# A two-layer diffusion step on one core: the engines' instruction order planned with the framework's other simulator

## The chip, the cores and the metric

One core of a Trainium2 chip runs the whole program. The metric is the device time of one execution in microseconds, the median over several runs; lower is better.

## The reference

One inference step of a hybrid diffusion backbone in float32 with two layers, the first with differential attention, the second with multi-head latent attention. 1024 latent tokens (`x_sample`) attend to themselves and to 256 cached tokens; 256 context tokens (`x_prompt`) attend to themselves alone. Both layers have 8 heads, a model width of 1024, RMS norms around them and an adaptive shift, scale and gate.

```python
for i in range(DEPTH):                       # DEPTH = 2
    hc = rmsnorm(x_ctx, g_pre[i]) * (1 + sc_c) + sh_c
    hl = rmsnorm(x_lat, g_pre[i]) * (1 + sc_l) + sh_l
    if kind == 0:                            # differential attention
        q, k, v, gate = split(h @ da_w_in)   # rope on q, k of the latents; cached k, v appended
        p = softmax(q k^T * scale)           # two score maps per head
        w = p[:, :, 0] - lam * p[:, :, 1]
        o = rmsnorm(w @ v, g_sub) * (1 - lam_init) * silu(gate)
    else:                                    # multi-head latent attention
        q_a, kv_a, k_pe, gate = split(h @ mla_w_in)
        q = rmsnorm(q_a, g_qa) @ w_qb ;  k, v = rmsnorm(kv_a, g_kva) @ w_kvb
        o = softmax([q_nope, q_pe] [k_nope, k_pe]^T * scale) @ v * silu(gate)
    x = x + gate_i * rmsnorm(o @ w_out[i], g_post[i])
```

It returns both streams and the new keys, values and latents of the context tokens.

## The kernel before

Each float32 operand of a large product is split into a high part and a remainder, and `mm3` (L320 on) issues three TensorE products for one: high by high (L323), and the two mixed ones (L324, L325). Weights come in through SyncE's queue (L313), ScalarE makes the high part (L315), and GpSimd or VectorE the remainder (L316; L355 and L356 for the query and key weights of the first layer). The 1280 rows are five pairs of 128-row tiles, four of latents and one of context tokens.

The time falls into five stages, which the text below calls A to E:

- A: norms and transposes of the inputs (`norm_pair_to_hT`, L286 to L295), the adaptive parameters, and the query, key and first value projections of layer 1 (`l0_qk_item`, `l0_tok_item`).
- B: the heads of layer 1 (`l0_heads`). A unit of work is one 128-row tile of one head, nine of them per head, 72 in all. `l0_scores` computes two score maps in PSUM tiles `S` (L594) and `pj` (L602), takes their maximum (L596) and the exponentials (L608, L610); `l0_weigh` mixes the two maps (L639); `p_transpose` transposes them (L662) and splits them into `pth` and `ptl` (L664, L665); `l0_values` multiplies with the values (by `mm3`) and stores through L699. The scores are recorded two units ahead of the weights. Between them a `Feeder` records further projections (values, gates, adaptive parameters, the first chunks of the gated output).
- C: the output projection of layer 1 (`out_items`, `residual`), the norms and transposes of layer 2 (L286 to L295 again) and its input projections (`l1_items`).
- D: the heads of layer 2 (`l1_heads`), 80 units: scores (`l1_scores`, L1255 to L1259), maximum and exponential (L1270 to L1274), transposes and splits as before, values (`l1_values`, L1297, L1298), with the projections of the next head between them.
- E: the output projection of layer 2 and the final sums (L980, L986).

The kernel is recorded, not issued: leaving the tile context hands the whole list to the framework's planner. The planner runs the list through a simulator of the core. Whenever that simulator can take another instruction on an engine, the planner gives it the earliest recorded one whose inputs and buffers are free at that simulated moment; later recorded work passes work that is not ready. What comes out is one fixed order for every engine and for every queue that issues transfers, with semaphores between them. On the chip each engine keeps to its order.

So the order in which the program is recorded sets priorities, and the planner's simulated clock sets who overtakes whom. How finely two recorded streams can mix is visible in one loop of `l0_heads`:

```python
for w in f[:2]:
    next(turns)          # transposes and splits of this unit
    feed(w)              # projection work, as much as the weight w allows
    next(sc, None)       # scores two units ahead
```

No line of the kernel fixes the order by hand beyond this: there are no explicit semaphores and no manual dependencies.

## Time and profile before

| | |
|---|---|
| median of 3 runs | 2020.48 us (2020.45 to 2022.48) |
| the profiled execution, own time | 2026.26 us |
| its span, first to last instruction | 2024.3 us |
| mean granted TensorE clock | 0.985 |
| TensorE busy, weight loads busy | 1925.5 us, 1729.8 us |
| VectorE, ScalarE, GpSimd busy | 1255.1, 965.1, 520.4 us |
| bytes moved by DMA | 225.05 MB, mean 111 GB/s |

The profiled execution is 5.8 us longer than the median. The profile counts an instruction as busy from its start to its end; matmuls are pipelined, so consecutive ones overlap and the busy time of TensorE is the union of them. Idle time of an engine is put down to what released the instruction that ended it.

### The profile page before, as it was taken

How to read it: one execution, taken by the hardware profiler on the slowest of the kernel's cores; microseconds unless marked ns; L12 is line 12 of the kernel's file. 1: busy time of each engine (PE TensorE's matmuls, PEld its weight loads, DVE VectorE, ACT ScalarE, POOL GpSimd, SP SyncE). 2: the span in 40 equal slices, each digit the busy share in tenths (PEclk: the TensorE clock that was granted, in tenths of full speed). 3: DMA queues.
4: the chain of work that ended last, by engine and by line, in shares of the span. 5: the costliest groups of instructions: out<-in, count | busy, mean ns of one | idle time of the engine just before them, and what ended most of it. 6: DMA issues, size and time to landing. Idle time of an engine off the chain costs nothing. (4 is left out here: it accounts for less than half of the span.)

```text
span 2024.3 us, 36143 instructions
## 1 busy us (share of the span) xinstructions
PE 1925.5 (95%) x13472; PEld 1729.8 (85%) x13472; DVE 1255.1 (62%) x2511; ACT 965.1 (48%) x2421; POOL 520.4 (26%) x741
## 2 busy tenths in 40 slices
PE   6899999999999999999988899999999999999998
PEld 4788888798989787888888898888999889998998
DVE  4544456788878787898337533247766876777413
ACT  4421223567666666667345523234554444545421
POOL 3354443213122212223334431011000110003214
PEclk8999999999999999999999999999999999999999
DMA  8455643544455454456434312210100001013412
GB/s 307 143 164 184 189 158 131 159 132 139 125 148 170 127 160 130 132 161 192 152 110 129 97 35 74 81 42 26 31 28 28 22 26 39 27 38 94 150 62 104
DMA packets 211440, 225.05 MB, mean 111 GB/s; under 512 B 24033, under 2 KB 175937, under 8 KB 211137
## 3 DMA queue, kind: packets, MB, share of 16 engines
q1 hardware_dynamic: 210960, 222.70, 35.6%
q8 instruction: 106, 1.74, 0.4%
q14 instruction: 70, 0.57, 0.1%
q10 hardware_dynamic: 304, 0.05, 0.0%
HBM read 153.14 MB, written 69.53 MB: 110 GB/s over the span
## 5 line engine op out<-in xcount | busy, mean ns | idle before, releaser
L323 PE MATMUL pj<-wh,hh 128*128 128x256 f32 (+1 forms) x1264 | 370.4, 293 | 8.9 <-DVE ptl L665 3.5
L324 PE MATMUL pj<-wl,hh 128*128 128x256 f32 (+1 forms) x1264 | 360.8, 285 | 6.1 <-DVE wl L316 3.7
L325 PE MATMUL pj<-wh,hl 128*128 128x256 f32 (+1 forms) x1264 | 360.3, 285 | 1.7 <-POOL hl L295 1.6
L316 POOL TENSOR_TENSOR wl<-wst,wh 128x512 fp32r<-128x512 f32 (+3 forms) x98 | 113.0, 1161 | 582.2 <-ACT wh L315 485.8
L323 PEld LDWEIGHTS pj<-wh,hh 128*128 128x128 f32 x1264 | 243.6, 193 | 14.4 <-DVE ptl L665 4.1
L324 PEld LDWEIGHTS pj<-wl,hh 128*128 128x128 f32 x1264 | 243.9, 193 | 8.2 <-DVE wl L316 4.1
L325 PEld LDWEIGHTS pj<-wh,hl 128*128 128x128 f32 x1264 | 243.3, 193 | 4.3 <-POOL hl L295 3.0
L325 PE MATMUL pj<-hh,wl 128*128 128x512 f32 (+1 forms) x512 | 188.5, 368 | 0.6 <-POOL wl L356 0.5
L323 PE MATMUL pj<-hh,wh 128*128 128x512 f32 (+1 forms) x512 | 188.3, 368 | 0.0
L324 PE MATMUL pj<-hl,wh 128*128 128x512 f32 (+1 forms) x512 | 187.8, 367 | 0.0
L596 DVE TENSOR_REDUCE mA<-S 128x1 f32<-128x1024 f32 x128 | 155.5, 1220 | 48.1 <-PE S L594 47.1
L608 ACT ACTIVATE e<-S,bias 128x1024 f32<-128x1024 f32 x128 | 142.9, 1116 | 79.5 <-DVE bias L605 79.5
L594 PE MATMUL S<-kl,q 128*128 128x512 f32 x512 | 149.3, 411 | 6.0 <-ACT e L608 5.6
L664 ACT CAST pth<-tp 128x512 fp32r<-128x512 f32 (+1 forms) x208 | 99.4, 512 | 82.9 <-PE tp L662 81.7
L664 ACT CAST pth<-pj 128x512 fp32r<-128x512 f32 (+1 forms) x192 | 98.4, 519 | 74.4 <-PE pj L662 71.6
L665 DVE TENSOR_TENSOR ptl<-tp,pth 128x512 fp32r<-128x512 f32 (+1 forms) x208 | 116.2, 582 | 14.1 <-ACT pth L664 13.3
L639 DVE SCALAR_TENSOR_TENSOR e<-e,cf,e 128x512 f32<-128x512 f32 (+1 forms) x192 | 123.6, 687 | 1.1
L665 DVE TENSOR_TENSOR ptl<-pj,pth 128x512 fp32r<-128x512 f32 (+1 forms) x192 | 113.3, 594 | 12.6 <-ACT pth L664 12.1
L315 ACT CAST wh<-wst 128x512 fp32r<-128x512 f32 (+3 forms) x140 | 78.5, 573 | 79.1 <-issue 21.8
L325 PEld LDWEIGHTS pj<-hh,wl 128*128 128x128 f32 x512 | 96.3, 188 | 20.6 <-POOL wl L356 3.6
L324 PEld LDWEIGHTS pj<-hl,wh 128*128 128x128 f32 x512 | 96.3, 188 | 16.9
L662 PE MATMUL pj<-identr,e 128*128 128x128 f32 x640 | 106.5, 277 | 4.2 <-DVE s L496 1.2
(331 smaller groups left out, 5281.6 us busy)
## 6 DMA issues: line engine op xcount, KB each, us to landing
q<-qsd SPq DMA_DIRECT2D x320, 64.0 KB, 2.2
wst<-in_da_w_in_dram SPq DMA_DIRECT2D x64, 256.0 KB, 3.4
kl<-ksd SPq DMA_DIRECT2D x64, 192.0 KB, 3.8
wst<-in_w_out_dram SPq DMA_DIRECT2D x48, 256.0 KB, 3.7
ast<-in_w_ada_dram SPq DMA_DIRECT2D x8, 1024.0 KB, 9.1
wh<-in_w_ada_dram SPq DMA_DIRECT2D x32, 256.0 KB, 4.2
wl<-in_w_ada_dram SPq DMA_DIRECT2D x32, 256.0 KB, 5.3
vdh<-s SPq DMA_DIRECT2D x24, 256.0 KB, 2.0
```

Source lines behind the costliest of these rows:

```text
L315: nc.scalar.copy(wh, st)
L316: (lo_engs or [nc.gpsimd])[k0 // kb % len(lo_engs or [0])].tensor_tensor(out=wl, in0=st, in1=f32(wh), op=ALU.subtract)
L323: nc.tensor.matmul(out, a[0], b[0], start=first, stop=False)
L324: nc.tensor.matmul(out, a[0], b[1], start=False, stop=False)
L325: nc.tensor.matmul(out, a[1], b[0], start=False, stop=last)
L594: nc.tensor.matmul(S[:, so:so + 512], st(cc, o), kl[cc][:, so:so + 512], start=(o == 0), stop=(o == 1))
L596: nc.vector.reduce_max(out=mA[:, cc:cc + 1], in_=S, axis=AX.X)
L608: nc.scalar.activation(u.es[cc][:, 0:1024], A[cc], AF.Exp, bias=bias[:, cc:cc + 1], scale=0.125, accum_out=u.zA[:, cc:cc + 1])
L639: nc.vector.scalar_tensor_tensor(out=w[:, sl], in0=w[:, sl], scalar=cf, in1=e0[:, sl], op0=ALU.mult, op1=ALU.add)
L662: nc.tensor.transpose(tp[:, j, :], u.e[:, (c0 + j) * P:(c0 + j + 1) * P], self.ident)
L664: nc.scalar.copy(hi, tp[:, 0:cn, :])
L665: nc.vector.tensor_tensor(out=u.ptl[g][:, 0:cn, u.i * P:(u.i + 1) * P], in0=tp[:, 0:cn, :], in1=f32(hi), op=ALU.subtract)
```

## The change

One argument is given where the tile context is made. The planner then makes its order with the framework's other simulator, which prices instructions and keeps them in flight by a different model: in the framework's words, it plans "against TimelineSim instead of CoreSim". The recorded list, the tiles, the pools with their numbers of buffers and the arithmetic are the same. The order on every engine, the order in every DMA queue, the assignment of buffers and the places of the semaphore waits all come out of the planner, and are made anew.

```diff
-    with tile.TileContext(nc) as tc:
+    with tile.TileContext(nc, schedule_with_timeline_sim=True) as tc:
         tile_diffmla_kernel(tc, ins, outs)
```

## The prediction, made before the result was known

> **What bounds the kernel now.** I read the page's first two parts, then busy time by stage, then TensorE's waits stage by stage, then the timeline of single matmuls. A change within 0.2%, about 4 us, I count as none: a measurement of this kernel can hardly tell less.
>
> The page first: the span, the busy times, and TensorE's busy tenths and granted clock over 40 slices.
>
> ```profile
> span 2024.3 us, 36143 instructions
> PE 1925.5 (95%) x13472; PEld 1729.8 (85%) x13472; DVE 1255.1 (62%) x2511; ACT 965.1 (48%) x2421; POOL 520.4 (26%) x741
> ...
> PE   6899999999999999999988899999999999999998
> ...
> PEclk8999999999999999999999999999999999999999
> ```
>
> TensorE is the bound nearly everywhere, and it idles 2024.3 - 1925.5 = 98.8 us. The same by stage, in the order A to E of the section on the kernel (columns: busy time of each engine in the stretch, with counts, then the granted clock):
>
> ```profile
> 0.00:342.00 342.00, 315.74 (x1743) 261.54 (x1744) 160.60 (x257) 95.42 (x186) 146.95 (x145) 0.97 0.56 187
> 342.00:965.00 623.00, 599.93 (x4341) 530.93 (x4339) 508.89 (x1000) 408.81 (x1073) 152.20 (x269) 0.99 0.51 147
> 965.00:1345.00 380.00, 356.06 (x2561) 331.41 (x2560) 147.92 (x258) 149.94 (x378) 117.04 (x181) 0.97 0.30 92
> 1345.00:1890.00 545.00, 529.09 (x3783) 482.13 (x3782) 399.39 (x934) 272.90 (x663) 64.41 (x95) 1.00 0.11 34
> 1890.00:2024.30 134.30, 124.69 (x1052) 123.76 (x1050) 38.28 (x63) 38.00 (x124) 39.77 (x53) 0.97 0.34 116
> ```
>
> TensorE's idle time is 26.3, 23.1, 23.9, 15.9 and 9.6 us in A to E. VectorE, the next in line, reaches 508.89 / 623 = 82% in B and 73% in D, so it does not set the time on average, but it has little room there.
>
> What the order decides is visible in the timeline of TensorE in B, around 602 us (start, duration, group):
>
> ```profile
> 602.42 0.60 PE L662 MATMUL pj<-identr,e 128*128 128x128 f32 x4
> 602.77 0.37 PE L323 MATMUL pj<-wh,hh 128*128 128x256 f32 x1
> 602.97 0.28 PE L324 MATMUL pj<-wl,hh 128*128 128x256 f32 x1
> 603.09 0.28 PE L325 MATMUL pj<-wh,hl 128*128 128x256 f32 x1
> 603.21 1.09 PE L594 MATMUL S<-kl,q 128*128 128x512 f32 x4
> ...
> 1010.78 0.28 PE L323 MATMUL pj<-wh,hh 128*128 128x256 f32 x1
> 1010.90 0.28 PE L324 MATMUL pj<-wl,hh 128*128 128x256 f32 x1
> 1011.01 0.28 PE L325 MATMUL pj<-wh,hl 128*128 128x256 f32 x1
> ```
>
> Four transposes, three matmuls of a projection, four scores: two streams are mixed at a grain of some 0.4 us. In C around 1010 us there is one stream alone, and the matmuls start every 0.12 us without a gap. There no other order of the same matmuls can be faster or slower.
>
> **The change, part by part.** It adds and removes no arithmetic: the same 13472 matmul records of the same shapes, the same 2511 of VectorE, the same transfers. The time in which matmuls stream therefore stays (about 1925 us busy), and the whole effect lies in the 98.8 us of idle time, and in whatever new idle time a new order makes. I take the stages one by one, with TensorE's waits in B, C and D (total us, number, longest):
>
> ```profile
> PE S L594 <- ACT e L608: 5.6, 8, 2.8
> PE pj L189 <- DMA wh<-in_w_ada_dram: 3.8, 3, 2.3
> PE pj L323 <- DVE ptl L665: 3.7, 6, 1.3
> PE pj L685 <- ACT oT L682: 2.1, 3, 1.3
> ...
> PE pj L662 <- PE pj L189: 0.2, 1, 0.2
> ...
> PE xt L286 <- ACT hfull L293: 10.0, 5, 3.4
> PE pj L759 <- POOL xt L748: 4.2, 1, 4.2
> PE pj L324 <- DVE wl L316: 3.7, 2, 3.3
> ...
> PE tp L323 <- DVE ptl L665: 4.1, 5, 1.5
> PE tp L1255 <- DVE ptl L665: 3.3, 2, 2.0
> PE pj L323 <- DVE vl L1195: 2.4, 4, 1.6
> ...
> PE tp L1214 <- DVE knl L1154: 0.2, 1, 0.2
> ```
>
> Stages A and E. A's idle time is mostly the first transfers and the first norms, where nothing else is ready to be put ahead; E is one stream of products and a tail of sums. I take 0 for both. What hides a changed order there is the backlog of ready projection matmuls. If that cover fails, a stage pays a wait like the longest single ones shown, 4.2 us; the same is the most that a luckier order gains in each, since the start stays. So A and E are 0, between -8 and +8.
>
> Stage B. TensorE stops 35 times there for 22.3 us in all (17 rows, the first and the last quoted): a unit's score matmuls stand at the head of its queue while ScalarE still reads the PSUM tile, or a matmul waits for VectorE's split `ptl`. Stage D has 24 such stops of 15.7 us (10 rows, first and last quoted), nearly all for VectorE's results. Together 59 stops in 72 + 80 = 152 units, 38.0 us, 0.64 us each. Each is a place where the planner's clock said "ready" and the chip was a little later, or where nothing at all was ready. A planner with another clock puts such places elsewhere. Bounds: it loses all of them, -38 us; or it makes twice as many, +38 us. For a value between these ends I go by the nearest row, which is the mean stop, and by how few there are: in about six units out of ten there is one stop, in the others none. Where a unit runs without a stop, a displaced instruction can only make one; where it has one, a displaced instruction can remove it or move it. A random displacement thus finds more places to harm than to help, at 93 units against 59. With a displacement effective in one unit out of three, that is 93 / 3 = 31 made and half of 59 / 3, some 10, removed: 21 more stops, 21 x 0.64 = 13 us. I take +13. One third is my choice; the two ends above hold whatever the share is.
>
> Stage C. The 10.0 us for `hfull` come from norms and transposes of layer 2 that follow one another through VectorE and ScalarE (L293, L294, L295); the single stops of 4.2 and 3.7 us are the hand-over from B to C and the weights split there. These are chains more than matters of order. I take 0, with -10 (the waits for `hfull` filled with projection work) and +10 (as many again).
>
> DMA queues. SyncE's queue is also put in a new order, and a wait at its head holds the transfers behind it. The queue's own waits:
>
> ```profile
> SPq L1298 <- DVE yT L1297: 234.1, 25, 18.4
> SPq L313 <- POOL wl L316: 191.5, 61, 34.9
> SPq L699 <- POOL y L698: 130.5, 38, 5.8
> ```
>
> The first stands before a store of D's results, up to 18.4 us, the second before a weight load that needs its buffer, up to 34.9 us. A weight load recorded behind such a store is late by that much, and covered as long as the projections run on other weights; in B only one row of TensorE's waits ends with a transfer, 3.8 us for the adaptive weights. I take 0, with -4 (that row gone) and +10 (three loads late by the 3.3 us of the longest wait for a weight, `wl` L316).
>
> GpSimd and ScalarE, at 26% and 48%, gain or lose idle time which costs nothing unless it ends in one of the stops above.
>
> The sum is 0 + 13 + 0 + 0 = +13 us. On the profiled execution, 2026.3 us with a span of 2024.3, this gives 2039; against the median of 2020.5, which is 5.8 us less, 2033.5. I give the time against the median: 2033.
>
> [...]
>
> ```profile
> 1250.00:1300.00 50.00, 50.00 (x263) 42.51 (x262) 11.85 (x15) 14.79 (x30) 5.15 (x4) 1.00 0.29 84
> 1050.00:1100.00 50.00, 37.31 (x275) 35.62 (x274) 39.79 (x71) 28.40 (x74) 23.74 (x26) 0.90 0.44 141
> 900.00:950.00 50.00, 44.42 (x319) 39.90 (x319) 44.88 (x82) 36.69 (x93) 20.72 (x28) 0.98 0.60 183
> ```
>
> [...]
>
> The second row shows the clock: with 12.7 us idle in 50 the granted clock was 0.90, while B and D keep 0.99 and 1.00 with their 59 short stops. [...]
>
> **Rivals.** First, the other side: *the new order fits the chip better*. Then the scores and `ptl` waits go where ready projection work is put ahead of them. For it: the stops are short, 0.64 us, and 0.4 us of projection (three matmuls) already fits between two steps, so one or two groups more would cover each. Against it: in D the projections are few, and the stops there end with VectorE, at 73%. Half of the 38 us gone gives 2020.5 - 19 = 2001. It decides from the point where the removed stops outnumber the new ones.
>
> Second, *nothing to measure*: in A, E and most of C the queue is one stream, and what changes in B and D cancels. For it: removed and new stops are of one size. Against it: to stay within 4 us the two numbers may differ by no more than six. 2020.5.
>
> Third, *the projections run early*. The order may put projection matmuls ahead of attention wherever both are ready, and B's last heads then run without them. In B they are the filler:
>
> ```profile
> L323 PE MATMUL pj<-wh,hh 128*128 128x256 f32 x525 | 154.8, 295 | 3.9 <-DVE ptl L665 3.5
> ```
>
> 525 groups of three at 0.12 us are 184 us of the 600 that TensorE is busy, so attention alone is about 5.5 us a unit and VectorE's share 508.89 / 72 = 7.1. In a head of nine units without projections VectorE sets the pace, at 9 x 1.6 = 14 us of idle TensorE. A milder price is the row from 900 to 950 us above: VectorE 44.88 of 50, TensorE idle 5.6 us. For it: that row, which shows what B looks like where the filler thins out. Against it: projections need PSUM tiles `pj`, which attention shares, so they cannot run far ahead. Two to three heads give some 35 us: 2055.
>
> **How the numbers follow.** Forecast (more short stops, 2024.5 to 2047): 0.38. Better fit (around 2001): 0.34; I give it that much because both signs are open in the argument on places, which rests on my one third. Nothing to measure: 0.16. Projections early (around 2055): 0.12. So faster 0.34, same 0.16, slower 0.38 + 0.12 = 0.50. The range reaches down through most of the better fit, to 2020.5 - 26 (19 in B and D, and 7 of the bounds of C and the transfers) = 1994, and up to 2062, past the early projections by the upper half of what C can add; about one case in ten is left out on each side. The forecast's own range is 2024 to 2047.
>
> **What would show it.** The same numbers of matmuls and of VectorE instructions, and TensorE busy within some 5 us of 1925 (right on the work). In B and D more stops than 35 and 24, of about 0.6 us, ended by `e` L608, `ptl` L665 and VectorE's results (right on the place); fewer, and the better fit is right. Idle time bunched in B's last heads with VectorE over 85% speaks for early projections. A changed stage A, long waits of TensorE for weights or `wst`, or a clock below 0.97 in B would show that I was wrong on the place. The prediction is most likely wrong if the other simulator's clock is nearer to the chip's than the one in use, which nothing in the trace of before can tell.

## The result, and the profile after

The changed kernel takes 2148.86 us (median of 4, 2145.32 to 2150.69) against 2021.16 us beside it: 1.063 times the time, interval 1.0616 to 1.065. The forecast was 2033, with 2062 as the upper end. The sign was right; the size was ten times too small.

The page of the changed kernel (span, busy times, TensorE's busy tenths, its granted clock):

```profile
span 2148.7 us, 36207 instructions
...
PE 1958.2 (91%) x13472; PEld 1757.1 (82%) x13472; DVE 1252.3 (58%) x2511; ACT 966.0 (45%) x2421; POOL 524.9 (24%) x741
...
PE   5999999898998988898898999999899998998798
...
PEclk9999999899999999999899999999999999999999
```

The work is the same: 13472 matmuls, 2511 instructions of VectorE. The span grew by 124.4 us: TensorE's idle time from 98.8 to 2148.7 - 1958.2 = 190.5 us (+91.7), and its busy time by 32.7 us for the same matmuls.

To compare stages I cut both traces at the same events, the start of the first and the end of the last 1024-wide exponential of each layer's heads, which both kernels have (the prediction's cuts of the kernel before lie up to 13 us away). Busy time by stage, A to E, of the kernel before (columns as in the prediction):

```profile
0.00:330.00 330.00, 305.12 (x1665) 251.69 (x1666) 153.41 (x243) 88.97 (x170) 146.95 (x145) 0.97 0.55 185
330.00:959.00 629.00, 604.55 (x4371) 536.37 (x4371) 510.58 (x1003) 410.61 (x1075) 151.06 (x268) 0.99 0.50 147
959.00:1358.00 399.00, 372.98 (x2681) 345.15 (x2680) 163.58 (x296) 158.56 (x401) 121.09 (x187) 0.97 0.31 93
1358.00:1888.00 530.00, 516.17 (x3696) 470.79 (x3695) 387.67 (x903) 267.92 (x651) 61.49 (x88) 1.00 0.12 35
1888.00:2024.00 136.00, 126.69 (x1069) 125.76 (x1067) 39.86 (x69) 39.01 (x130) 39.77 (x53) 0.97 0.34 115
```

and of the changed one:

```profile
0.00:321.00 321.00, 295.39 (x1659) 246.21 (x1660) 154.48 (x243) 89.72 (x171) 149.35 (x145) 0.99 0.56 189
321.00:1044.00 723.00, 637.49 (x4392) 562.38 (x4390) 508.49 (x1002) 407.54 (x1073) 159.18 (x270) 0.95 0.44 131
1044.00:1425.00 381.00, 367.54 (x2684) 342.43 (x2683) 160.69 (x295) 158.88 (x402) 119.47 (x186) 0.98 0.30 93
1425.00:1999.00 574.00, 526.21 (x3667) 475.47 (x3668) 387.26 (x902) 270.41 (x649) 60.67 (x88) 0.99 0.11 32
1999.00:2149.00 150.00, 131.60 (x1076) 130.60 (x1074) 41.37 (x70) 39.42 (x129) 36.24 (x53) 0.93 0.29 104
```

With the marks read to a tenth of a us, A changed by -9.2, B by +94.9, C by -18.2, D by +43.3 and E by +13.6 us, together the 124.4. In B the clock fell from 0.99 to 0.95, and TensorE is busy 33 us more there. VectorE is busy 508 / 723 = 70% there, so its amount of work does not set the time.

TensorE's waits in B (325 to 1050 us, the first two rows of 33) and in D (1410 to 2011 us, the first three of 17):

```profile
PE pj L323 <- DVE ptl L665: 18.1, 17, 2.1
PE pj L662 <- DVE ptl L665: 13.6, 16, 5.7
...
PE tp L1255 <- DVE ptl L665: 11.5, 14, 1.2
PE tp L323 <- DVE ptl L665: 9.2, 14, 1.1
PE tp L662 <- DVE ptl L665: 8.6, 14, 2.2
```

The splits `ptl`, a releaser that the prediction named, end 36 of the 87 us of waits in that stretch of B; the other one, `e` (L608), hardly grew (at `S`, L594, 5.6 us before and 6.0 here). Counting every stop of TensorE from 0.15 us on in these cuts: B had 36 (23.6 us) and has 107 (84.7 us), D had 21 (13.5 us) and has 71 (47.2 us). In B the stops longer than 1 us went from 6 (10.0 us in all) to 25 (47.0 us).

The longest, 5.7 us, shows how one comes about. TensorE around it (start, duration, group, and in brackets the idle time before it with its releaser):

```profile
485.13 0.63 PE L602 MATMUL pj<-kl,q 128*128 128x256 f32 x4
491.45 0.66 PE L662 MATMUL pj<-identr,e 128*128 128x128 f32 x2 [5.68 <-DVE ptl L665]
492.04 0.55 PE L323 MATMUL pj<-pth,vh 128*128 128x256 f32 x1
492.39 0.42 PE L324 MATMUL pj<-ptl,vh 128*128 128x256 f32 x1
...
497.80 0.28 PE L323 MATMUL pj<-pth,vh 128*128 128x256 f32 x1
497.92 0.28 PE L324 MATMUL pj<-ptl,vh 128*128 128x256 f32 x1
```

and VectorE at the same time:

```profile
484.42 1.23 DVE L596 TENSOR_REDUCE mA<-S 128x1 f32<-128x1024 f32 x1 [0.47 <-PE S L594]
485.56 3.41 DVE L639 SCALAR_TENSOR_TENSOR e<-e,cf,e 128x512 f32<-128x512 f32 x3
488.89 1.21 DVE L596 TENSOR_REDUCE mA<-S 128x1 f32<-128x1024 f32 x1
490.03 0.68 DVE L603 TENSOR_REDUCE m<-pj 128x2 f32<-128x512 f32 x1
490.63 1.27 DVE L665 TENSOR_TENSOR ptl<-pj,pth 128x512 fp32r<-128x512 f32 x2
```

The transposes need the `pj` tiles that `ptl` frees. ScalarE's half of that split is done by 485.8 us (the trace has `pth`, L664, from 484.67 for 1.09 us), but VectorE first mixes the next unit (L639, 3.41 us) and takes two maxima (L596, L603): `ptl` comes only at 490.63. In TensorE's fixed order no projection stands here to fill the time; a run of them without a break has just been spent, from 476.81 to 481.71 us. Then the second cost: after the stop the matmuls start 0.21 us apart instead of 0.12, until 497.5 us.

### The profile page after: what moved, and what is told of

Same layout as the page of the kernel before. It is cut to its first block, busy times and chain, and to the rows that moved or that the text cites. A ratio compares the mean times of both kernels' runs of the same rounds, so it can differ in the third digit from the quotient of the medians.

```text
span 2148.7 us, 36207 instructions
## 1 busy us (share of the span) xinstructions
PE 1958.2 (91%) x13472; PEld 1757.1 (82%) x13472; DVE 1252.3 (58%) x2511; ACT 966.0 (45%) x2421; POOL 524.9 (24%) x741
## 4 chain that ended last, share of the span: by engine, by line
PE 40%; DVE 9%; issue 3%; ACT 3%; DMA 3%; POOL 2%; SPq 0%; POOLq 0%; ACTq 0%; DVEq 0%
PE pj L323 7%; PE pj L324 7%; PE pj L325 7%; PE tp L323 3%; PE tp L325 3%; PE tp L324 3%; DVE ptl L665 2%; PE tp L662 2%; DVE mm L1265 2%; DMA yst<-yTd 1%; PE S L1256 1%; PE S L1255 1%; PE S L1257 1%; PE S L1258 1%; PE S L1259 1%
## 5 line engine op out<-in xcount | busy, mean ns | idle before, releaser
L323 PE MATMUL pj<-wh,hh 128*128 128x256 f32 (+1 forms) x1264 | 362.9, 289 | 11.4 <-ACT y L688 4.3
L325 PE MATMUL pj<-wh,hl 128*128 128x256 f32 (+1 forms) x1264 | 358.3, 285 | 0.0
L323 PEld LDWEIGHTS pj<-wh,hh 128*128 128x128 f32 x1264 | 242.1, 192 | 18.9 <-DVE hh L294 6.2
L325 PEld LDWEIGHTS pj<-wh,hl 128*128 128x128 f32 x1264 | 241.9, 192 | 2.4 <-issue 0.8
L608 ACT ACTIVATE e<-S,bias 128x1024 f32<-128x1024 f32 x128 | 142.9, 1116 | 138.4 <-DVE bias L605 138.4
L323 PE MATMUL pj<-hh,wh 128*128 128x512 f32 (+1 forms) x512 | 187.6, 368 | 0.0
L325 PE MATMUL pj<-hh,wl 128*128 128x512 f32 (+1 forms) x512 | 186.5, 367 | 0.0
L596 DVE TENSOR_REDUCE mA<-S 128x1 f32<-128x1024 f32 x128 | 155.1, 1216 | 48.6 <-PE S L594 48.6
L664 ACT CAST pth<-tp 128x512 fp32r<-128x512 f32 (+1 forms) x208 | 100.7, 509 | 148.0 <-PE tp L662 146.8
L594 PE MATMUL S<-kl,q 128*128 128x512 f32 x512 | 145.1, 412 | 6.5 <-ACT e L608 6.0
L664 ACT CAST pth<-pj 128x512 fp32r<-128x512 f32 (+1 forms) x192 | 97.8, 527 | 77.2 <-PE pj L662 72.1
L247 POOL TENSOR_SCALAR orsv<-oss 128x2 f32<-128x2 f32 x40 | 9.1, 226 | 497.1 <-ACT oT L692 497.0
L662 PE MATMUL pj<-identr,e 128*128 128x128 f32 x640 | 103.4, 280 | 28.1 <-DVE ptl L665 13.6
L323 PE MATMUL pj<-pth,vh 128*128 128x256 f32 x336 | 104.7, 312 | 25.7 <-DVE ptl L665 15.9
L639 DVE SCALAR_TENSOR_TENSOR e<-e,cf,e 128x512 f32<-128x512 f32 (+1 forms) x192 | 124.5, 692 | 0.7
L594 PEld LDWEIGHTS S<-kl,q 128*128 128x128 f32 x512 | 90.1, 192 | 32.6 <-ACT e L608 15.3
```

Source lines behind the costliest of these rows:

```text
L323: nc.tensor.matmul(out, a[0], b[0], start=first, stop=False)
L325: nc.tensor.matmul(out, a[1], b[0], start=False, stop=last)
L594: nc.tensor.matmul(S[:, so:so + 512], st(cc, o), kl[cc][:, so:so + 512], start=(o == 0), stop=(o == 1))
L596: nc.vector.reduce_max(out=mA[:, cc:cc + 1], in_=S, axis=AX.X)
L608: nc.scalar.activation(u.es[cc][:, 0:1024], A[cc], AF.Exp, bias=bias[:, cc:cc + 1], scale=0.125, accum_out=u.zA[:, cc:cc + 1])
L639: nc.vector.scalar_tensor_tensor(out=w[:, sl], in0=w[:, sl], scalar=cf, in1=e0[:, sl], op0=ALU.mult, op1=ALU.add)
```

## The experiments

Most kernels here hold chosen engines to a stored order. After the recording, each stored pair of neighbours gets an order-only edge, and the planner makes everything that is not pinned anew around it (shortened: the decoding of the stored lists is left out):

```diff
+def keep_order(nc, tc):
+    info = mybir.DependencyInfo(mybir.DependencyClass.NoSync, mybir.DependencyReason.DATA)
+    for seq in ORDERS.values():              # one list of instructions per engine
+        for a, b in zip(seq, seq[1:]):
+            tc.add_manual_dep(b, a.name, info, reason="keep_order")
...
         tile_diffmla_kernel(tc, ins, outs)
+        keep_order(nc, tc)
```

The edges themselves cost nothing that can be measured: a kernel below with TensorE and VectorE pinned (and 235 matmuls moved a little) takes 0.9997 of the time of the kernel before. But an engine that is not pinned does not keep its old order. In the third kernel below, with TensorE pinned, VectorE's list has the same line and tiles as in the kernel before at only 903 of its 2511 places. "From before" and "from after" name the source of a pinned order; stages are cut at the marks above, B and D beside 629 and 530 us before, 723 and 573 after.

**Which engine's order carries the loss.** In each of the first four, one part of one kernel is given the other's order.

The changed kernel with TensorE's order from before:

> The changed kernel with TensorE's order alone put back to that of the kernel before (a chain of order-only edges through its 13328 matmuls); every other engine and queue is still ordered by the other simulator. Theory 1 (TensorE's order is what costs: long runs of projection matmuls delay the attention steps, and VectorE's results come late in consequence): most of the loss gone, 2020 to 2045 us, stops in the layer-1 heads back to some 35 to 50, clock there 0.98 to 0.99. Rival 1 (VectorE's and ScalarE's own orders put the split ptl behind less urgent work): 2100 us or more, since those orders stay. Rival 2 (the DMA queue's order): 2100 or more.

2134.93 us, ratio 1.0574 (1.0538 to 1.061). Its stages B and D:

```profile
330.00:1064.00 734.00, 635.11 (x4368) 552.46 (x4367) 512.37 (x1002) 411.66 (x1073) 156.53 (x270) 0.97 0.44 127
...
1462.00:1991.00 529.00, 516.32 (x3703) 471.24 (x3702) 385.89 (x906) 268.06 (x651) 61.00 (x88) 1.00 0.12 35
```

D is healed entirely, B not at all (734), and the gain of C is gone (398). Theory 1, that TensorE's order is the cause, fell as it stood: it had 2020 to 2045 us. D's loss and C's gain hang on TensorE's order; B's loss does not need it.

The changed kernel with VectorE's, ScalarE's and GpSimd's orders from before:

> The changed kernel with the orders of VectorE, ScalarE and GpSimd put back to those of the kernel before; TensorE and the DMA queues are still ordered by the other simulator. Theory 1: most of the loss stays, 2090 to 2150 us, with ptl and e as the releasers of TensorE's stops. Rival 1: 2020 to 2050 us. Rival 2: above 2100.

2180.1 us, 1.0795 (1.0763 to 1.0826): worse than the change itself, and above the range of theory 1. B 718.5, D 589.3. VectorE has exactly its order from before here, so B's loss does not need VectorE's new order either. Each of the two is enough.

The kernel before with TensorE's order from after:

> The kernel before (planned with the first simulator) with TensorE's order alone taken from the changed kernel. Theory 1: the loss appears, 2110 to 2160 us. Rival 1: 2020 to 2060 us, since VectorE and ScalarE are ordered by the first simulator. Rival 2: 2020 to 2060.

2144.47 us, 1.0616 (1.0581 to 1.0652). Its stages B and D:

```profile
337.00:1034.00 697.00, 620.36 (x4388) 551.44 (x4386) 505.49 (x1003) 407.02 (x1075) 158.51 (x269) 0.96 0.46 135
...
1420.00:1992.00 572.00, 523.27 (x3662) 471.77 (x3662) 391.43 (x900) 269.99 (x646) 60.48 (x87) 0.99 0.11 32
```

With TensorE's order from after, D loses as much as with the change (572 against 573 us) and B 68 us of the 95. VectorE's order was made anew around it here, so these 68 us are not shown to be TensorE's alone; that TensorE's order can spoil B without VectorE's is shown by the second kernel.

The changed kernel with SyncE's order from before:

> The changed kernel with the order of SyncE's DMA queue alone put back to that of the kernel before. Rival 2 (loads and stores in another order): 2020 to 2060 us. Theory 1 and rival 1: 2120 to 2160 us, no change beyond a few us, since TensorE's stops are ended by VectorE and ScalarE and hardly any by a transfer.

2155.37 us, 1.0688 (1.0636 to 1.0741), B 728.7, D 572.0: the order of SyncE's queue is not the cause of their loss. E is 142.3 us here, against 150 in the changed kernel.

**Both together, and what is left.** The changed kernel with TensorE's and VectorE's orders from before:

> The changed kernel with the orders of TensorE and VectorE put back to those of the kernel before; ScalarE, GpSimd and the DMA queues are still ordered by the other simulator. Theory 1 as amended (in the layer-1 heads two orders each cost the same stretch: TensorE's runs of projections, and VectorE's mixing of the two maps, L639, put ahead of the maxima of the next scores): 2020 to 2045 us, that stage back from 734 to 630 to 645 us. Rival 3 (the loss in that stage with TensorE's order put back comes from ScalarE or the DMA queue): 2100 us or more.

2049.1 us, 1.0135 (1.0108 to 1.0162), just above the range of the theory. B is 629.5 again and D 533.9. C is 411 us, and there its wait for the norms is longer than before's 10.0 us:

```profile
PE xt L286 <- ACT hfull L293: 14.1, 4, 6.0
```

All four engines pinned to the order from before, the other simulator planning only the transfers:

> The changed kernel with the orders of TensorE, VectorE, ScalarE and GpSimd all put back; only the DMA queues and the semaphore waits that follow from them are the other simulator's. Theory 1 as amended: 2015 to 2035 us. Rival 2 in what is left of it (the DMA queue's order costs once the engines' orders fit): 2050 us or more.

2025.63 us, 1.0024 (1.0009 to 1.004): the queues' new order by itself is worth some 4 to 5 us, no more. The 23 us between this kernel and the one above go with ScalarE's and GpSimd's orders, 13 of them in C (411 against 398).

**VectorE's part.** The kernel before, TensorE's order its own, with VectorE's order as in the first experiment:

> The kernel before, planned with the first simulator, with TensorE's order its own and VectorE's order alone taken from the run with TensorE put back (e1): no order of TensorE, only VectorE's differs on purpose. Theory 1 as amended: the layer-1 heads lose as in e1, 700 to 735 us against 628, the layer-2 heads keep their 530, in all 2090 to 2135. Rival 3: 2020 to 2040.

2159.97 us, 1.0689 (1.0667 to 1.0712), B 747.1, D 531.0: above the range of the theory. With TensorE's order fixed, VectorE's order does to B more than the whole change. What in it? The two lists of VectorE differ most in the mixing (L620 to L639). The next kernel is the one before, TensorE's and VectorE's orders pinned, with only these 416 of VectorE's 2511 instructions at the places of the first experiment. One place of VectorE's list:

```diff
-L639 e<-e,cf,e 128x512
+L639 e<-e,cf,e 128x512 x2
+L639 e<-e,cf,e 128x256
 L596 mA<-S
 L596 mA<-S
 L603 m<-pj
-L639 e<-e,cf,e 128x512
 L496 s<-s,s
 L604 m<-m,mA
-L639 e<-e,cf,e 128x256
```

> The kernel before with one group of VectorE's instructions moved: the mixing of the two score maps in the layer-1 heads (reciprocals, factor and the 64 x 3 products, L627 to L642) stands where the other simulator put it (as in e1), all the rest of VectorE and all of TensorE in the order of before. Theory: this group ahead of the maxima is the whole of the loss that VectorE's order makes there, 720 to 745 us in the layer-1 heads, 2100 to 2145 in all. Rival 4 (many small displacements of VectorE add up, this group a part of them): 2040 to 2090.

2125.18 us, 1.0515 (1.0497 to 1.0534). Its stage B, and the first rows of TensorE's waits there:

```profile
330.00:1061.00 731.00, 636.33 (x4373) 553.16 (x4371) 506.63 (x1002) 411.76 (x1074) 152.83 (x269) 0.96 0.42 127
```

```profile
PE S L594 <- ACT e L608: 29.0, 24, 7.2
PE pj L662 <- DVE ptl L665: 18.0, 19, 3.2
```

103 us in B from the places of 416 instructions, with TensorE's order unchanged, while VectorE's own work stays at 507 us. The maxima (L596, L603) stand behind the mixing; the exponentials wait for the bias that comes from them; the score tile `S` is freed late, and the scores at the head of TensorE's queue wait (5.6 us before, 29.0 here). The waits for `ptl` grow as well, from 4.8 to 32.4 us in B. ScalarE's wait for that bias in B, before, here and in the changed kernel:

```profile
ACT e L608 <- DVE bias L605: 79.5, 52, 4.5
```

```profile
ACT e L608 <- DVE bias L605: 120.6, 46, 5.4
```

```profile
ACT e L608 <- DVE bias L605: 138.4, 51, 5.4
```

So the mechanism on VectorE is shown for this order: urgent short instructions queued behind a non-urgent block. In the changed kernel the wait for the bias is as long, but TensorE's wait for `S` stays at 6.0 us; there the delay arrives through `ptl`. The worked example above is a case of it, and one case only.

**TensorE's part.** One number per engine is set in the next kernels: how many instructions the other simulator commits to an engine ahead of the running one, its issue window, and with it how far the plan lets TensorE run ahead. The number at which the changed kernel is planned stands in no run; the kernels here set 12 for the other engines each time and differ in TensorE's. With 1 for TensorE, once free and once with VectorE pinned to its order from before (the edit in short):

```diff
+    hw_specs.TRN2Spec.ENG_ISSUE_QUEUE_DEPTH = {PE: 1, the others: 12}
     with tile.TileContext(nc, schedule_with_timeline_sim=True) as tc:
```

> [...] Theory 2 (TensorE's runs of projections, and of scores ahead of transposes, come from that window, VectorE's mixing does not): the layer-2 heads go from 573 back to 525 to 540 us, the layer-1 heads keep a loss (700 to 740), in all 2095 to 2135. Rival 5 (the window does not matter, the simulated durations make the order): 2130 to 2165, layer-2 heads at 560 or more.

2399.07 us, 1.1847 (1.1812 to 1.1882). B 793.8, D 701.9.

> As e10, and VectorE's order put back to that of the kernel before. Theory 2: both causes gone, 2015 to 2050 us. Rival 5: above 2090.

2334.9 us, 1.154 (1.1515 to 1.1564). B 776.3, D 676.5. Theory 2 failed both times: at 1 both stages are far worse than in the changed kernel, so the changed kernel's window is not simply too large. The theory was amended: at 1 the simulated TensorE is too slow, in the changed kernel it commits too early, and the best lies between. Two larger values follow. At 12 the amended theory had 690 to 720 us for B, 535 to 560 for D, and 2085 to 2130 in all:

> [...] Rival 5 (the window plays no part above a few): 2140 to 2155 us.

2092.98 us, 1.034 (1.0322 to 1.0358). B 691.0, D 550.0.

> The same with a window of 4. Theory 2 as amended: layer-2 heads 530 to 560 us, in all 2080 to 2130 us. Rival 5: 2140 to 2160 us. If it is nearer to the window of 1, the simulated TensorE is still too slow at 4: above 2170 us.

2069.99 us, 1.0224 (1.0205 to 1.0243). Its stages B and D:

```profile
327.00:1008.00 681.00, 615.47 (x4357) 543.88 (x4355) 503.60 (x1001) 406.31 (x1072) 166.71 (x270) 0.97 0.47 137
...
1393.00:1923.00 530.00, 512.60 (x3687) 473.98 (x3688) 386.06 (x906) 268.84 (x652) 60.00 (x88) 0.99 0.12 35
```

The series 1, 4, 12 gives D 702, 530, 550 and B 794, 681, 691, against 573 and 723 in the changed kernel. At 4 D's loss is gone. From 4 to 12, where TensorE's number is all that changes, D gets 20 us longer and B 10, so how far the plan believes TensorE to run ahead has a part in the loss. 53 us of B's loss stay at 4. The number moves every engine's order, so the series does not say which engine's order does it.

What in TensorE's order does it? In B the projections (L323 to L325 on `wh` and `wl`) of the kernel with TensorE's order from after come in fewer and longer runs, 117 of 14.0 matmuls in the mean against 169 of 9.7. My candidate was that they are spent elsewhere and no longer stand between a unit's last transposes and its values, where they cover the split `ptl`. The kernel before with 235 projection matmuls, in 23 places, moved out of that gap to just ahead of the last transposes, VectorE pinned:

> The kernel before with 235 projection matmuls of TensorE's order moved a little: in 23 places of the layer-1 heads, where they stood between a unit's last transposes and its value products, they are put in front of those transposes; VectorE's order stays that of before. Theory 3 (TensorE loses in these heads because the projections no longer lie between the transposes and the values that wait for ScalarE and VectorE): 23 stops more, released by ptl, of 0.6 to 1.1 us each as in the changed kernel: 2035 to 2050 us. Rival 6 (the place of the projections inside a unit does not matter, only the total): 2018 to 2027 us.

2021.21 us, 0.9997 (0.9981 to 1.0012): nothing.

```profile
327.00:951.00 624.00, 603.93 (x4374) 535.81 (x4373) 506.30 (x1000) 408.85 (x1072) 150.67 (x268) 1.00 0.50 148
```

B has 20 us of idle time, against 24. That theory fell. Which feature of TensorE's order costs B and D their time stays open; moving only the scores of D, or all of B's projections, was not tried.

**A better one.** C is shorter with TensorE's order from after. So the kernel before, with the 2662 matmuls between the last scores of layer 1 and the first of layer 2 in the order from after (1526 stand at another place), the rest pinned to its own:

> The kernel before, planned with the first simulator, with TensorE's order its own except between the layer-1 and the layer-2 heads (2662 matmuls), where it is the changed kernel's. If the 18 us that the changed kernel gained in that stage come from TensorE's order there (projections put ahead of the transposes that wait for hfull): 2003 to 2014 us, idle time of that stage from 26 to some 14 us. If they come from work left over from the stage before, or from the other engines: 2018 to 2025 us.

2010.62 us, 0.9949 (0.993 to 0.9969). The waits of C, against 10.0 us for `hfull` before:

```profile
PE pj L324 <- DVE wl L316: 9.3, 4, 6.1
...
PE xt L286 <- ACT hfull L293: 0.9, 2, 0.6
```

The norms' wait is filled with projections, and part of it comes back as a wait for split weights. The same with the 1576 matmuls of stage A too (584 at another place):

> As e8, with TensorE's order of the changed kernel also in the first stage, up to the first scores (1576 matmuls): that stage was 9 us shorter in the changed kernel, at the same idle time. If TensorE's order makes it: 1998 to 2008 us. If the 9 us come from the clock's state or from work moved into the next stage: 2006 to 2016 us.

2004.21 us, 0.992 (0.9903 to 0.9937). Its stages A and C:

```profile
0.00:323.00 323.00, 295.15 (x1663) 247.99 (x1664) 154.73 (x242) 89.68 (x170) 148.04 (x145) 0.99 0.56 189
...
952.00:1341.00 389.00, 370.99 (x2686) 344.76 (x2685) 163.14 (x297) 157.16 (x403) 122.95 (x188) 0.98 0.31 96
```

A is 7 and C 10 us shorter than before, and the heads are as before: the best kernel here, 18 us faster than the one before beside it (2022.17). The two gains differ in kind. C's is mostly idle time that went (18 us, 26 before). A's idle time did not fall (27.9 us, 24.9 before); its busy time did, by 10 us, at a granted clock of 0.99 against 0.97.

## Why the prediction was right or wrong

**The work stays, stops decide: half right.** The counts of instructions are the same and more than half of the new stops wait for `ptl`, as named (from 18 to 84 in B and D); `e` (L608) hardly counts. But "TensorE busy within some 5 us of 1925" failed: 1958.2. And two of the signs that were to show the place wrong came: the clock in B is below 0.97 (0.948), and stage A changed.

**B and D, +13: the step that failed.** The term had three factors. The place was right for `ptl`. The length of a stop, 0.64 us, was near in D (47.2 / 71 = 0.66) and low in B (84.7 / 107 = 0.79). The number was wrong: 21 more stops forecast, 178 - 57 = 121 measured. Even the upper bound, twice as many stops or +38 us, was no bound: the idle time in B and D rose by 61 + 34 = 95 us. It took the 59 stops of the kernel before as a measure of how exact a planner's clock is, and let one displacement in three units act. It also read the stops wrongly where it says that about six units out of ten have one: 59 of 152 are four in ten, and six in ten have none, as its own 93 against 59 says. The experiments show no share of displaced instructions but two orders, either of which spoils B: +103 us from VectorE's mixing with TensorE's order fixed, +90 with VectorE's order fixed and TensorE's new, and 95 in the changed kernel, where both are new. They do not add. In D, TensorE's order is the one. Nor did I look at VectorE's order at all as a place for the error: at 82% it has "little room", I wrote, and took that as a matter of its busy time. Its order was enough.

**The clock: wrongly left out.** I saw B and D keep 0.99 and 1.00 with their 59 stops, of 0.64 us in the mean, and put nothing into the sum for it. B's clock, 0.948 over 723 us against 0.995 over 629, means 38 - 3, some 34 us of full speed withheld, and the busy time of B rose by about as much (33 us; 32.7 over all stages), a quarter of the whole loss. The two need not be the same: with the mixing displaced the clock withheld 26 - 3, some 22 us in B, and the busy time rose by 32. In B the loss of clock goes with stops over 1 us, but not with their number alone: 6 of them before at 0.995, 25 in the changed kernel at 0.948, 28 with the mixing displaced at 0.965; and D of the second experiment has 22 at 0.996. I reasoned from the mean stop, and the new order made long ones and close ones. In slices of 20 us, 17 of 35 in B have a granted clock of 0.93 or less in the changed kernel, 2 of 31 in the one before. Two such slices and one untouched:

```profile
480.00:500.00 20.00, 14.32 (x86) 13.19 (x85) 12.56 (x23) 10.95 (x26) 6.14 (x8) 0.83 0.64 178
800.00:820.00 20.00, 15.05 (x71) 7.22 (x70) 11.80 (x23) 10.32 (x29) 7.68 (x10) 0.83 0.52 159
640.00:660.00 20.00, 18.95 (x140) 17.04 (x138) 13.56 (x27) 13.51 (x39) 5.85 (x12) 1.00 0.22 66
```

The first holds the stop of 5.68 us. The clock records of both traces hold 0.5 and 1 alone, and the matmul starts 0.21 and 0.12 us apart go with them. Around that stop the record has half rate from 490.79 to 497.62 us, 6.83 us long; another half-rate stretch, shown below, is 3.41 us long. B's stops went from 36 to 107, and the falls to half rate there from 2 to 18.

**C, 0 between -10 and +10:** 18 us shorter, outside the bounds. I called these waits chains, which an order can hardly change; the low bound, the `hfull` waits filled, is what happened: idle time fell by 12.5 us, and busy time by 5.4. **A:** -9, just past its bound of 8. **E:** +14, past it too. One stop for `yT` (L1386) is 8.9 us of it; where SyncE's queue has its order from before and the rest is planned around it, that stop is 0.7 us and E is 142.3. With TensorE's order from before E is 139.5. The rest was not taken apart. **DMA queues, 0:** right for the queues by themselves, 4 to 5 us; in E, beside the other new orders, they seem to cost more.

**The rivals.** *Better fit* was true of A and C alone. *Nothing to measure* fell. *Projections early* named a second mechanism of the right sign and size (+35), but its signs in the profile, VectorE over 85% and idle time bunched in B's last heads, did not come: VectorE is at 70%, and TensorE's tenths are 8 and 9 throughout B. Its price was also too high: (600 - 184) / 72 is 5.8 us a unit, not 5.5, which makes 12 us a head and not 14.

## What to carry to other kernels

An order planned by a model is a parameter like any other: measure it stage by stage, and pin the better one per stage, since one order won in A and C and lost in B and D. When an order changes, ask for each engine what short, urgent instruction now stands behind a long one that nobody waits for; an engine at 70% can hold up the one at 95%. The stops that a kernel has do not bound those that another order can make: 57 became 178 here, more than the 152 units.

## What was not expected of the hardware

A stop can be far shorter than the half-rate stretch that follows it. In one of the kernels with a window of 1 (VectorE pinned), a stop of 0.94 us before 558.46 is followed within a microsecond by a half-rate stretch, in which the matmuls start 0.21 us apart:

```profile
558.46 0.39 PE L323 MATMUL pj<-pth,vh 128*128 128x256 f32 x1 [0.94 <-DVE ptl L665]
...
559.67 0.42 PE L325 MATMUL pj<-pth,vl 128*128 128x256 f32 x1
...
562.65 0.32 PE L324 MATMUL pj<-ptl,vh 128*128 128x256 f32 x1
...
563.04 0.28 PE L324 MATMUL pj<-ptl,vh 128*128 128x256 f32 x1
```

The matmuls were not idle when the rate fell; it fell 0.8 us into the next run. The clock records tell more: in the traces of the kernel before and of the changed one, all 23 and all 55 changes of the rate lie on a grid of 3.41 us. The same place cut at that grid (columns as in the prediction; the granted clock is the third number from the end):

```profile
555.92:559.33 3.41, 1.66 (x12) 1.46 (x13) 3.41 (x9) 0.37 (x1) 0.00 (x0) 1.00 0.61 178
559.33:562.74 3.41, 3.41 (x18) 3.41 (x18) 2.21 (x7) 3.11 (x8) 0.00 (x0) 0.50 0.15 44
562.74:566.15 3.41, 3.25 (x28) 3.04 (x28) 1.30 (x4) 1.75 (x9) 0.00 (x0) 1.00 0.00 0
```

TensorE was busy for 1.66 of 3.41 us before the fall, with two stops of about 1 us. In B of the changed kernel all 18 falls to half rate follow a grid step in which TensorE was busy 67% or less, and no step at full rate with less than 51% was followed by another at full rate; in between both happen. So in B of the changed kernel it is the busy share of such a step that goes with the fall, and in the stretch above two stops of about 1 us came before one.

And three mixing products of the same shapes took 1.81 us in one stretch of the kernel before (from 498.38 us) and 3.41 us in the one of the changed kernel shown above. GpSimd was idle in the first, and in the second it was at work on a weight remainder:

```profile
483.83 4.20 POOL L316 TENSOR_TENSOR wl<-wst,wh 128x512 fp32r<-128x512 f32 x3 [1.81 <-ACT wh L315]
```

In the changed kernel the 128x512 products (L639) take 0.75 us in the mean, at most 0.76, where GpSimd is idle (88 of them), and 0.91 us, at most 1.77, where it works at the same time for 0.1 us or more (39). No run was made to test it.
